# Seven block products for eight in the up-projections of a two-layer hybrid decoder, with weight sums made by adding DMAs

## The chip, the cores and the metric

The kernel runs on one core of one Trainium2 chip. Times are device microseconds of one execution of the whole program. The time before is 1455.77 us, the median of 3 runs (1455.77 to 1455.92). All arithmetic is float32; a matrix product is made of three passes in a rounded format, as told below.

## The reference, cut to what matters

Two decoder layers over 512 tokens of width 1024. Layer 0 mixes tokens by dilated window attention, layer 1 by a gated linear recurrence (LRU). After each mixer follows a gated feed-forward block, which the change is about:

```python
D_MODEL, SEQ, D_FF = 1024, 512, 3 * 1024

def rms_norm(x, g):
    return x * rsqrt(mean(x * x, axis=-1) + 1e-6) * g

def conv_ffn(x, w_up, conv_w, conv_b, w_down):          # w_up: 1024 x 6144
    u = causal_dwconv(x @ w_up, conv_w, conv_b)         # three taps over the tokens
    g, v = u[..., :D_FF], u[..., D_FF:]
    return (gelu(g) * v) @ w_down

for layer in range(2):
    h = mixer(rms_norm(x, norm_mix_pre[layer]))
    x = x + rms_norm(h, norm_mix_post[layer])
    h = conv_ffn(rms_norm(x, norm_ffn_pre[layer]), ...)
    x = x + rms_norm(h, norm_ffn_post[layer])
```

The product x @ w_up has two halves: 3072 features that go through gelu (gate) and 3072 that multiply them (value).

## The kernel before

The order of all work on each engine is the order in which the program writes it. Normalised activations stand transposed in SBUF as `hT`, 8 blocks of 128 input features by 512 tokens, split in two parts: `hi`, rounded to the matmul's format, and `lo`, the rest. Weights are split the same way. A product takes three passes, listed in `PASSES`: hi x hi, hi x lo, lo x hi (`mm3`, L259).

The up-projection of a layer (`ffn`) goes through 12 chunks j. For each j a chunk of 256 gate features and one of 256 value features is loaded (`w_cols`), 1 MB each. A chunk makes two tiles of 128 features by 512 tokens. For one tile, `feat` runs over 8 blocks of input features and 3 passes, 24 matmuls of 512 columns into one PSUM bank; chunk 0 of a layer does it in two halves of 256 columns, since the first tokens are ready earlier. `sink` then empties the bank: `conv` reads it three times, once on ACT (L596) and twice on DVE (L600, for the two shifted taps); a gate tile then gets its gelu on ACT (L611), a value tile is multiplied into it on DVE (L615). The down-projection (`rows_proj`) follows.

What feeds the matmuls is `pump`. A list `plan` holds all weight chunks of the program in order of use. Three buffers (`RAW_BUFS`) hold raw chunks; `load` issues the next load on SP's queue (L199) when one is free. `pump` cuts a raw chunk into pieces and splits each: ACT writes `whi` (L149), DVE writes `wlo` (L150), both 128 partitions by 512 elements at a time. At most 8 split units (`W_UNITS`) are alive. `tick`, called after every tile, pumps one or two pieces and advances the `side` generators, which hold work spread over several tiles, such as the norms. Since ACT and DVE work their queues in order, a split that waits for its data holds what is queued behind it.

`x_sb` holds the residual stream x in SBUF, 2 MB; `postnorm` adds to it after a projection. `gain` holds rows of norm gains, two buffers. PSUM has eight banks of 128 x 512, given out in turn.

Of the kernel before, what the change touches and what calls it, by code (L numbers as in the profile page):

```python
# [31 lines left out]

W_UNITS = 8
RAW_BUFS = 3
GEN_BUFS = 32
TOE_BUFS = 2
CP_PAD = 8
WARM = 5

SHORT_ORDER = [  # L40
# [34 lines left out]
def kernel(  # L75
# [29 lines left out]
    htp = ctx.enter_context(tc.tile_pool(name="htp", bufs=1))  # L105
    wp = ctx.enter_context(tc.tile_pool(name="wp", bufs=W_UNITS))
    gp = ctx.enter_context(tc.tile_pool(name="gp", bufs=GEN_BUFS))
# [6 lines left out]
    def nm(s):  # L114
        uid[0] += 1
        return f"{s}{uid[0]}"
# [13 lines left out]
    make_identity(nc, ident)  # L130
    x_sb = cp.tile([P, 4, D], F32, tag="x_sb", name="x_sb")

# [19 lines left out]
    plan = []  # L152
    state = {"dma": 0, "cv": 0, "live": 0, "next": 0, "hold": False}
    raws, units, pieces = {}, {}, []
    sides, first_w, first_y, one = [], [], [], []

    def parts_of(kind, raw):
# [7 lines left out]
        return [raw]  # L165

    def pump(limit=2):

        for _ in range(limit):
            i = state["cv"]  # L170
            if not pieces and i < state["dma"]:
                pieces.extend((i, j, u) for j, u in enumerate(parts_of(plan[i][0], raws.pop(i))))
                state["cv"] += 1
            if pieces and state["live"] < W_UNITS:
                i, j, raw = pieces.pop(0)
                hi, lo = (
                    wp.tile([P] + list(raw.shape[1:]), F32R, tag=t, name=nm("w" + t)) for t in ("hi", "lo")
                )
                h = raw.shape[1] // 2
                cuts = [(slice(None), slice(0, h)), (slice(None), slice(h, 2 * h))]  # L180
                if raw.shape[1] == 1:
                    cuts = [(slice(None), slice(0, 1), slice(n, n + 512)) for n in (0, 512)]
                if plan[i][4] is not None:
                    split_normed(hi, lo, raw, plan[i][4] + (2 * j if plan[i][0] == "value" else 0))
                    cuts = []
                for c in cuts:
                    split(hi[c], lo[c], raw[c])
                units[i, j] = (hi, lo)
                state["live"] += 1
            while not pieces and state["dma"] < len(plan) and state["dma"] - state["cv"] < RAW_BUFS:  # L190
                load()
# [17 lines left out]
    def take(i, j):  # L209
        while (i, j) not in units:  # L210
            before = state["live"]
            pump(1)
            assert before != state["live"]
        return units[i, j]

    def done(n=1):
        state["live"] -= n
# [4 lines left out]
    def tick():  # L222
        for s in list(sides):
            s[0] -= 1
            if s[0] <= 0:
                try:
                    s[0] = next(s[1])
                except StopIteration:
                    sides.remove(s)
        if not state["hold"]:  # L230
            pump(1 if state["live"] >= W_UNITS - 2 else 2)

# [3 lines left out]

    def w_cols(w, c0, normed=False):
# [4 lines left out]
        plan.append(("feat", KD, 256, srcs, 0 if normed else None))  # L242

# [71 lines left out]
    def prenorm(t, hT, g, wait):  # L315
        xh, gh = halves(x_sb[:, t, :]), halves(g)
# [31 lines left out]
    def first_transposed(t, i):  # L348

        ps = psum("tr")  # L350
        for k in range(4 * i, 4 * i + 4):
            nc.tensor.transpose(
                ps[:, k % 4 * P : (k % 4 + 1) * P],
                x_sb[:, t, i * 512 : i * 512 + 512].rearrange("t (p k) -> t k p", k=4)[:, k % 4], ident,
            )
        first_split(t, i, ps)
# [15 lines left out]
    def first_squares(i):  # L372
        for t in range(4):
            junk = gen(s="junk")
            nc.scalar.activation(
                junk, x_sb[:, t, i * 512 : i * 512 + 512], AF.Square, accum_out=first_ss[i][:, t : t + 1]
            )
# [22 lines left out]
    def postnorm(t, banks, g, final):  # L400
        at = [slice(0, 512), slice(512, 1024)]
        parts = banks
        u = [gen(s="post") for _ in at]

        def gained(i):
            nc.vector.tensor_tensor(u[i], parts[i], g[:, at[i]], op=ALU.mult)

        y = rms(parts, gained)
        for i, c in enumerate(at):
            xc = x_sb[:, t, c]  # L410
# [12 lines left out]
    def feat(W, hT, dst, n0, n1):  # L423
        for k in range(KD):
            mm3(
                dst[:, n0:n1],
                [w[:, k, :] for w in W],
                [h[:, k, n0:n1] for h in hT],
                k == 0,
                k == KD - 1,  # L430
            )

    def feat_tiles(n, hT, sink, halves=False):
# [15 lines left out]
        for c in range(n):  # L449
            i = chunk()  # L450
            for m in range(2):
                ps = psum()
                feat(take(i, m), hT, ps, 0, S)
                done()
                sink(2 * c + m, ps)
                tick()

# [17 lines left out]
    def rows_run(nchunks, A, prep, seq, order, post, pre, eng):  # L475
# [7 lines left out]
        def product(t, i, k, cols, start, stop):  # L483
            w = take(*W[k // 2][k % 2])
            c0 = i * 512
            mm3(
                banks[t][i][:, cols],
                [a[:, t * P : (t + 1) * P] for a in A[k]],
                [v[:, 0, c0 + cols.start : c0 + cols.stop] for v in w],
                start,  # L490
# [100 lines left out]
    def ffn(layer, hT, post, pre):  # L591
# [13 lines left out]
        gv = []  # L605

        def sink(b, ps, j):
            m = b % 2
            if b < 2:
                u = conv(ps, 2 * j + m)  # L610
                nc.scalar.activation(u, u, AF.Gelu_apprx_tanh)  # L611
                gv.append(u)
            else:
                u = conv(ps, 24 + 2 * j + m)
                nc.vector.tensor_tensor(gv[2 * j + m], gv[2 * j + m], u, op=ALU.mult)  # L615

        order = [([0, 1, 2, 3], range(9)), ([0], range(9, 12)), ([1], range(9, 12))]
        order += [([2, 3], [9]), ([2], [10, 11]), ([3], [10, 11])]
        prep, run = rows_proj(12, act_split(gv), order, post, pre)
        for j in range(12):  # L620
            if j == 11:
                prep(3)
            feat_tiles(2, hT, lambda b, ps: sink(b, ps, j), j == 0)
        return run()


    def attention(hT, post, pre):
# [50 lines left out]
        def first_values(vs):  # L678
# [4 lines left out]
            def product(t, u, which=range(6)):  # L683
                W = take(ids[u // 2], u % 2)
                steps = [(k, a, b) for a, b in PASSES for k in (2 * u, 2 * u + 1)]
                for n in which:
# [3 lines left out]
                        hT[a][:, k, t * P : (t + 1) * P],  # L690
                        W[b][:, k % 2, :],
                        start=u == n == 0,
# [22 lines left out]
            product(3, 1)  # L715
            done(2)
            first_split(2, 1, T[0])
# [8 lines left out]
            for t in range(4):  # L726
                product(t, 3)
                pump(1)
            done(2)
            for t in range(4):  # L730
# [14 lines left out]
        def values(vs, permute, midway=None):  # L745
# [6 lines left out]
            for t in range(4):  # L752
                banks[t] = psum("v")
                for u in range(4):
                    W = take(ids[u // 2], u % 2)
                    steps = [(k, a, b) for k in (2 * u, 2 * u + 1) for a, b in PASSES]
                    for k, a, b in steps:
                        mm(  # L758
                            banks[t],
                            hT[a][:, k, t * P : (t + 1) * P],  # L760
                            W[b][:, k % 2, :],
                            start=(k, a, b) == (0, 0, 0),
                            stop=(k, a, b) == (KD - 1, 1, 0),
                        )
                    if t == 3 and u % 2:
                        done(2)
                if permute:
# [189 lines left out]
    def lru(hT, post, pre):  # L957
# [19 lines left out]
        def gates(n):  # L977
            W = take(chunk(), 0)
            sg = {}
            for m in range(2):  # L980
                for gx in range(2):
                    ps = psum("gate")
                    for k in range(2):
                        mm3(ps, [w[:, 2 * gx + k, m * P : (m + 1) * P] for w in W], xs[2 * n + k], k == 0, k == 1)
                    j = 2 * n + m
# [78 lines left out]
    for layer in range(2):  # L1064
# [24 lines left out]
    def x_half(t, i):  # L1089
        c = slice(i * 512, (i + 1) * 512)  # L1090
        nc.sync.dma_start(x_sb[:, t, c], x[0, t * P : (t + 1) * P, c])

# [71 lines left out]
```

## Time and profile before

| | before |
|---|---|
| runs, us | 1455.77, 1455.92, 1455.77 |
| profiled execution: span, us | 1454.0 |
| granted TensorE clock | 0.999 |
| PE busy | 1445.0 us, 99% |
| DVE busy | 879.8 us, 61% |
| ACT busy | 675.9 us, 46% |
| POOL busy | 133.9 us, 9% |
| HBM read, written | 156.24 MB, 15.29 MB |

The page gives the profiled execution by its span, from the first to the last instruction; the median of the runs is 1.8 us (0.12%) above it. PE is the matmul engine, PEld its weight loads, which overlap with matmuls, DVE the vector engine, ACT the scalar engine, POOL GpSimd, SP the engine whose queue issues the weight loads. In a row for a group of instructions stand the line, engine and operation, the tiles (written <- read), shapes and count, then busy us in all and mean ns of one, then the engine's idle time ahead of them and what ended it. A row for a DMA ends with the size of one and the median us from issue to landing, where known.

### The profile page before, as it was taken

To read this page: it belongs to the slowest core of one execution; us is meant where nothing else is said; L and a number is where in the kernel's file an instruction comes from. 1 tells how busy PE (TensorE), PEld (TensorE's weight loads), DVE (VectorE), ACT (ScalarE), POOL (GpSimd) and SP (SyncE) were. 2 spreads that over 40 slices of the span, in tenths; PEclk is the share of its full clock that TensorE was granted. 3 is DMA by queue.
4 is the path that set the end of the run, shared out by engine and by line. 5 is a ranking of instruction groups with operands and counts; after the bars stand their busy time and mean duration, and the time that the engine had idled before them with its cause. 6 is when DMAs were issued, how large, how long until landed. Compare 5 with 4: busy or idle time off the path is not lost.

```text
span 1454.0 us, 18793 instructions
## 1 busy us (share of the span) xinstructions
PE 1445.0 (99%) x6861; PEld 1214.4 (84%) x6861; DVE 879.8 (61%) x1955; ACT 675.9 (46%) x1532; POOL 133.9 (9%) x275
## 2 busy tenths in 40 slices
PE   9999999999999999999999999999999999999998
PEld 7888888888888898888888888888898888888886
DVE  6767747474735975555564338769775555564333
ACT  7656636262615553343444335589453434444221
POOL 0340414040402100000000001000100000000000
PEclk9999999999999999999999999999999999999999
DMA  7653637372726343323323322432333233223201
GB/s 225 207 146 109 174 113 208 104 215 97 216 96 211 102 131 100 103 87 102 101 88 116 115 73 88 131 116 84 120 102 116 87 102 102 87 104 128 88 0 58
DMA packets 125364, 172.76 MB, mean 119 GB/s; under 512 B 8736, under 2 KB 102392, under 8 KB 125272
## 3 DMA queue, kind: packets, MB, share of 16 engines
q1 hardware_dynamic: 114280, 145.48, 31.0%
q0 software_dynamic: 10144, 25.04, 5.9%
q8 instruction: 54, 0.88, 0.2%
q10 hardware_dynamic: 848, 1.05, 0.2%
q14 instruction: 38, 0.31, 0.1%
HBM read 156.24 MB, written 15.29 MB: 118 GB/s over the span
## 4 chain that ended last, share of the span: by engine, by line
PE 93%; ACT 4%; DVE 3%; issue 1%; DVEq 0%; ACTq 0%
PE ps L259 55%; PE acc L259 24%; PE v L758 8%; PE v L688 1%; DVE xb L967 1%; PE O L909 1%; PE S L854 1%; PE S L808 1%; DVE wlo L150 1%; ACT sig L988 1%; ACT whi L149 1%; PE O L259 1%; PE tr L341 1%; ACT sig L1007 0%; ACT a L1005 0%
## 5 line engine op out<-in xcount | busy, mean ns | idle before, releaser
L259 PE MATMUL ps<-hT,whi 128*128 128x512 f32 (+1 forms) x2752 | 801.3, 375 | 0.0
L259 PEld LDWEIGHTS ps<-hT,whi 128*128 128x128 f32 x2752 | 503.6, 188 | 91.6
L259 PE MATMUL ps<-hT,wlo 128*128 128x512 f32 (+1 forms) x1376 | 515.3, 374 | 0.0
L150 DVE TENSOR_TENSOR wlo<-raw,whi 128x512 fp32r<-128x512 f32 x360 | 230.8, 686 | 187.2 <-ACT whi L149 187.1
L259 PEld LDWEIGHTS ps<-hT,wlo 128*128 128x128 f32 x1376 | 259.1, 188 | 46.5
L149 ACT ACTIVATE whi<-raw 128x512 fp32r<-128x512 f32 x360 | 204.6, 621 | 135.4 <-PE acc L259 121.0
L600 DVE SCALAR_TENSOR_TENSOR u<-ps,cols,u 128x511 f32<-128x511 f32 x192 | 143.8, 749 | 140.6 <-ACT u L596 137.2
L259 PE MATMUL acc<-whi,ahi 128*128 128x512 f32 x512 | 199.7, 390 | 0.0
L259 PE MATMUL acc<-whi,alo 128*128 128x512 f32 x512 | 199.4, 389 | 0.1
L259 PE MATMUL acc<-wlo,ahi 128*128 128x512 f32 x512 | 199.3, 389 | 0.0
L143 ACT ACTIVATE whi<-raw,first_w 128x128 fp32r<-128x128 f32 (+1 forms) x432 | 146.2, 425 | 56.6 <-PE ps L259 33.9
L596 ACT ACTIVATE u<-ps,cols 128x512 f32<-128x512 f32 x96 | 74.8, 779 | 210.0 <-PE ps L259 210.0
L144 DVE SCALAR_TENSOR_TENSOR wlo<-raw,first_w,whi 128x128 fp32r<-128x128 f32 (+1 forms) x432 | 139.5, 389 | 1.4 <-ACT whi L143 1.3
L259 PEld LDWEIGHTS acc<-whi,alo 128*128 128x128 f32 x512 | 96.1, 188 | 20.5 <-DVE alo L150 0.5
L259 PEld LDWEIGHTS acc<-whi,ahi 128*128 128x128 f32 x512 | 96.1, 188 | 19.8
L259 PEld LDWEIGHTS acc<-wlo,ahi 128*128 128x128 f32 x512 | 96.2, 188 | 19.8
L758 PE MATMUL v<-whi,hT 128*128 128x512 f32 x320 | 102.4, 393 | 0.0
L302 POOL DMA_DIRECT2D turned<-T x36 | 19.6, 547 | 763.4 <-DVE T L296 759.9
L309 POOL DMA_DIRECT2D ft<-turned x144 | 78.7, 554 | 39.6 <-issue 17.7
L758 PEld LDWEIGHTS v<-whi,hT 128*128 128x128 f32 x320 | 60.1, 188 | 12.3
L611 ACT ACTIVATE u<-u 128x512 f32<-128x512 f32 x48 | 30.3, 632 | 80.4 <-DVE u L600 80.4
L758 PE MATMUL v<-wlo,hT 128*128 128x512 f32 x160 | 62.3, 389 | 0.0
(171 smaller groups left out, 1010.7 us busy)
## 6 DMA issues: line engine op xcount, KB each, us to landing
raw<-in_ffn_w_up_dram SPq DMA_DIRECT2D x48, 1024.0 KB
raw<-in_attn_w_qkv_dram SPq DMA_DIRECT2D x67, 512.0 KB
raw<-in_ffn_w_down_dram SPq DMA_DIRECT2D x24, 1024.0 KB
raw<-in_lru_w_in_dram SPq DMA_DIRECT2D x8, 1024.0 KB
turned<-T POOLq DMA_DIRECT2D x28, 256.0 KB, 2.6
ft<-turned POOLq DMA_DIRECT2D x112, 64.0 KB, 5.8
vrows<-v SPq DMA_DIRECT2D x16, 256.0 KB
vp<-vrows SPq DMA_DIRECT2D x16, 256.0 KB
```

The source lines that it names most:

```text
L143: nc.scalar.activation(hi[:, k], raw[:, k], AF.Copy, scale=w)
L144: nc.vector.scalar_tensor_tensor(lo[:, k], raw[:, k], w, hi[:, k].bitcast(F32), op0=ALU.mult, op1=ALU.subtract)
L149: nc.scalar.activation(hi, raw, AF.Copy)
L150: nc.vector.tensor_tensor(lo, raw, hi.bitcast(F32), op=ALU.subtract)
L259: mm(dst, l[a], r[b], start=start and n == 0, stop=stop and n == 2)
L302: nc.gpsimd.dma_start(d, T)
L309: nc.gpsimd.dma_start(t[32 * c : 32 * c + 32].rearrange("j (b x) -> j b x", b=4), d.rearrange("(b j) (c x) -> c j b x", j=32, c=4)[c],)
L341: nc.tensor.transpose(ps[:, k * P : (k + 1) * P], xs[i][:, k * P : (k + 1) * P], ident)
L596: nc.scalar.activation(u, ps, AF.Identity, scale=cc[:, j : j + 1], bias=cc[:, 48 + j : 49 + j])
L600: nc.vector.scalar_tensor_tensor(u[:, d:], ps[:, : S - d], wc, u[:, d:], op0=ALU.mult, op1=ALU.add)
L611: nc.scalar.activation(u, u, AF.Gelu_apprx_tanh)
L758: mm(banks[t], hT[a][:, k, t * P : (t + 1) * P], W[b][:, k % 2, :], start=(k, a, b) == (0, 0, 0), stop=(k, a, b) == (KD - 1, 1, 0),)
```

## The change

For chunks 3 to 10 of both halves, in both layers (32 chunks of 48 matmuls of 512 columns), the product of the 1024 x 256 weights with the 512 tokens is done as two blocks by two by two: two groups of 128 output features, two halves of the input features (4 blocks of 128), two halves of the tokens (256). Instead of eight block products there are seven (Strassen's scheme in a form with sums of sums), each of 4 blocks x 3 passes = 12 matmuls of 256 columns. Five sides change with it:

* **Token sums.** Four combinations of the token blocks are made once per layer, in `token_sums`, a side generator that starts with chunk 1: `hi + lo` on POOL, four sums on DVE, splits on ACT and DVE. They need 2 MB and more of SBUF: x is written to memory, its place and that of the two gain rows are used for them, and `x_back` brings x back after chunk 10.
* **Weight sums.** Each chunk needs four blocks as they are or summed: `s1`, `s2`, `s3`, `s4` stand for sums made in place in the raw buffer by DMAs that add to their destination (`add_rows`, issued on POOL, 256 KB each, 512 bytes per row piece). `ahead` adds a block from memory onto another (S1), `across` adds the first block onto it (S2), `upper` makes S4 and S3. Four such DMAs per chunk. `stream` sets their order among the splits of successive chunks: each must come after the split that reads the old content and before the one that reads the sum.
* **Splits.** A chunk is split in seven pieces (S1, W12, W11, A22, S2, S4, S3) instead of four, of the same size. Units are counted in halves, 16 alive. A raw buffer is free when its chunk's S3 is split.
* **Chains.** `seven` writes products in slots; chunk n has its seven products at slots 7n + 0, 3, 4, 8, 9, 13, 19 (P5, P1, P3, P2, P6, P7, P4), so that up to three chunks overlap. `later` puts off what follows a product by one or two slots. Two PSUM banks collect a chunk: ACT copies an intermediate out twice and one back into PSUM negated, DVE makes two results of 256 columns in PSUM; then `finish` runs the same convolution as before. Empty slots at both ends are filled with quarters of ordinary tiles.
* **Elsewhere** units are lists of two halves instead of one tile; the instructions are the same.

Over the program 1536 matmuls of 512 columns are replaced by 2688 of 256 columns.

```diff
-W_UNITS = 8
+HALVES = 16
+SEVEN = range(3, 11)
+AT = {5: 0, 1: 3, 3: 4, 2: 8, 6: 9, 7: 13, 4: 19}
+HALF = ("s1", "w11", "w12", "a22", "s2", "s3", "s4")
...
+    def blocks(i):
+        raw = raws[i]
+        return {
+            n: raw[:, 4 * k : 4 * k + 4, m * P : m * P + P]
+            for n, m, k in (("w11", 0, 0), ("w12", 0, 1), ("s1", 1, 0), ("a22", 1, 1))
+        }
+    def add_rows(to, src):
+        nc.gpsimd.dma_start(to, src, accum_op=ALU.add)
+    def ahead(i):
+        add_rows(blocks(i)["s1"], plan[i][3][0][0][:, 4:8, P:256])
+    def stream(i0, n):
...
+            def upper(i=i):
+                x = blocks(i)
+                add_rows(x["w12"], x["s1"])
+                add_rows(x["w11"], plan[i][3][0][0][:, 0:4, P:256])
+            def across(i=i):
+                x = blocks(i)
+                add_rows(x["s1"], x["w11"])
+            for at, item in (
+                (-6.4, (None, lambda i=i: ahead(i))), (0, ("s1", "s1")), (0.2, (None, across)), (2, ("w12", "w12")),
+                (4, ("w11", "w11")), (4.2, (None, upper)), (6, ("a22", "a22")), (8, ("s2", "s1")),
+                (10, ("s4", "w12")), (12, ("s3", "w11")),
+            ):
...
+                    items.append((7 * c + at, item))
+        return [item for _, item in sorted(items, key=lambda x: x[0])]
...
-            while not pieces and state["dma"] < len(plan) and state["dma"] - state["cv"] < RAW_BUFS:
+            while state["dma"] < len(plan) and state["dma"] - state["used"] < RAW_BUFS:
                 load()
...
-        for j in range(12):
-            if j == 11:
-                prep(3)
-            feat_tiles(2, hT, lambda b, ps: sink(b, ps, j), j == 0)
+        for j in range(SEVEN[0]):
+            if j == 1:
+                side(token_sums(hT, T))
...
+        i = seven(hT, T, begin, i)
+        x_back()
+        prep(3)
...
+    def token_sums(hT, T):
+        d = dp.tile([P, 4, D], F32, name=nm("x_kept"))
+        nc.gpsimd.dma_start(d, X[0])
...
+            nc.gpsimd.tensor_tensor(o, hi.bitcast(F32), lo.bitcast(F32), op=ALU.add)
...
+            tt(b11, b11, b12, op=ALU.subtract)
+            tt(b12, b12, b22, op=ALU.subtract)
+            tt(b22, b22, b11, op=ALU.add)
+            tt(b21, b21, b22, op=ALU.subtract)
+            yield 1
+            for n, b in enumerate((b11, b22, b12, b21)):
+                split(homes[2 * n][k], homes[2 * n + 1][k], b)
...
+    LEFT = {5: ("s1", 1), 1: ("w11", 0), 3: ("s4", 1), 2: ("w12", 0), 6: ("s2", 1), 7: ("s3", 1), 4: ("a22", 1)}
+    def seven(hT, T, begin, before):
...
+                for k in range(4):
+                    for q, (wa, ha) in enumerate(PASSES):
+                        mm(
+                            y[b][:, 0:256], W[wa][0][:, k, :], right[n](ha, k), start=n in (1, 5) and k == q == 0,
+                            stop=k == 3 and q == 2, skip_group_check=True,
+                        )
+                done(1)
+                if n == 5:
+                    later(1, lambda: nc.scalar.activation(p5, c, AF.Copy))
+                elif n == 3:
+                    def seed():
+                        nc.scalar.activation(z, c, AF.Copy)
+                        nc.scalar.activation(c, a, AF.Copy, scale=-1.0)
+                    later(1, seed)
+                elif n == 6:
+                    later(1, lambda: nc.vector.tensor_tensor(y[0][:, 256:512], z, c, op=ALU.subtract))
+                    later(2, lambda: finish(b0, y[0], j))
+                elif n == 7:
+                    later(1, lambda: nc.vector.tensor_tensor(y[1][:, 256:512], c, p5, op=ALU.subtract))
+                elif n == 4:
+                    later(1, lambda: finish(b0 + 1, y[1], j))
...
+        at = {7 * n + AT[p]: f(p) for n, f in enumerate(chains) for p in AT}
+        after = chunk()
+        fill = quarters(before, 1, SEVEN[0] - 1, 3)
...
-            w_cols(ffn_w_up[layer], j * 256)
-            w_cols(ffn_w_up[layer], D_FF + j * 256)
+            for half in range(2):
+                w_cols(ffn_w_up[layer], half * D_FF + j * 256, kind="seven" if j in SEVEN else "feat")
```

More of the change, by code (lines that the diff above doesn't have):

```diff
@@ L165, in parts_of, with plain @@
         return [raw]
+    def plain(i, j, raw, last):
+        kind, k0 = plan[i][0], plan[i][4]
+        if kind == "rows":
+            cuts = [raw[:, :, n : n + 512] for n in (0, 512)]
+        else:
+            h = raw.shape[1] // 2
+            cuts = [raw[:, :h], raw[:, h:]]
+        norm = None if k0 is None else k0 + (2 * j if kind == "value" else 0)
+        return (i, j), lambda: cuts, norm, last
+    def blocks(i):
[4 more added lines that the diff above has]
+        }
@@ new lines, in refill @@
+    def refill():
+        i = state["cv"]
+        if i >= state["dma"]:
+            return
+        if plan[i][0] == "seven":
+            n = 1
+            while plan[i + n][0] == "seven":
+                n += 1
+            pieces.extend(stream(i, n))
+            state["cv"] += n
+        else:
+            if plan[i + 1 : i + 2] and plan[i + 1][0] == "seven":
+                pieces.append((None, lambda: ahead(i + 1)))
+            parts = parts_of(plan[i][0], raws[i])
+            pieces.extend(plain(i, j, r, j == len(parts) - 1) for j, r in enumerate(parts))
+            state["cv"] += 1
@@ L167, in pump @@
     def pump(limit=2):
         for _ in range(limit):
[L170 to L189, printed above, removed]
@@ L190, in pump @@
-            while not pieces and state["dma"] < len(plan) and state["dma"] - state["cv"] < RAW_BUFS:
+            if not pieces:
+                refill()
+            while pieces and pieces[0][0] is None:
+                pieces.pop(0)[1]()
+            if pieces and state["live"] + 2 - (pieces[0][0][1] in HALF) <= HALVES:
+                key, cuts, norm, last = pieces.pop(0)
+                cuts = cuts()
+                his, los = [], []
+                for n, raw in enumerate(cuts):
+                    hi, lo = (
+                        wp.tile([P] + list(raw.shape[1:]), F32R, tag=t, name=nm("w" + t)) for t in ("hi", "lo")
+                    )
+                    if norm is not None:
+                        split_normed(hi, lo, raw, norm + n * raw.shape[1])
+                    else:
+                        split(hi, lo, raw)
+                    his.append(hi)
+                    los.append(lo)
+                units[key] = (his, los)
+                state["live"] += len(cuts)
+                state["used"] += last
+                while pieces and pieces[0][0] is None:
+                    pieces.pop(0)[1]()
@@ L488, in product @@
                 [a[:, t * P : (t + 1) * P] for a in A[k]],
[L489 removed]
+                [v[i][:, 0, cols] for v in w],
                 start,
```

179 lines of the change are left out of this document (145 added, 34 removed).

## The prediction

> **What bounds the kernel now.** I read the busy shares first, then the chain that ended last, then the groups by shape, then the windows and the timeline of an up-projection.
>
> ```profile
> PE 1445.0 (99%) x6861; PEld 1214.4 (84%) x6861; DVE 879.8 (61%) x1955; ACT 675.9 (46%) x1532; POOL 133.9 (9%) x275
> PE 93%; ACT 4%; DVE 3%; issue 1%; DVEq 0%; ACTq 0%
> 510.00:764.00 254.00, 254.00 (x1181) 212.93 (x1180) 151.59 (x223) 107.38 (x177) 0.00 (x0) 1.00 0.31 101
> ```
>
> TensorE is busy for 99% of the span and is 93% of the chain. The third line is the window 510 to 764 us, nearly all of layer 0's up-projection: span, then PE, PEld, DVE, ACT and POOL busy, granted clock (1.00), DMA share (0.31) and GB/s (101). PE never rests; DVE works 60% of that stage, ACT 42%, POOL nothing. So only less TensorE time can shorten the stage, and the question is whether what is added elsewhere still fits beside it.
>
> A busy sum does not give the rate of matmuls that overlap; the chain in order of time does (start, us, count):
>
> ```profile
> 31.98 27.20 PE ps L259 x120
> 510.50 253.77 PE ps L259 x1176
> 500.13 5.75 PE ps L259 x48
> 902.35 2.87 PE ps L259 x24
> ```
>
> The first piece is all 512 columns wide: 27.20/120 = 0.2267 us per matmul. The last two are stretches where chunk 0 runs in two halves of 256 tokens: 5.75/48 = 0.1198 and 2.87/24 = 0.1196. The second piece is layer 0's remaining 120 narrow and 1056 wide ones, and fits: (253.77 - 120 x 0.1198)/1056 = 0.2267. A half-width matmul thus costs 53% of a wide one, about 13 ns on each being independent of width.
>
> **The TensorE term.** A chunk (256 output features of one half) now takes 48 wide matmuls: 48 x 0.2267 = 10.88 us. As seven products it takes 7 x 12 = 84 narrow ones: 84 x 0.1198 = 10.06 us, 1.44 us per product. Both layers have 32 such chunks: 1536 wide matmuls go (348.2 us), 2688 narrow come (322.0 us): **-26.2 us**. That is 7.5% of those matmuls and not the eighth that the count suggests. The Trainium skill, "TensorE: Matmul & The Clock Gate", section "Back-to-back issue gap", has width/2.4 + 2.5 ns, an estimate of 109 and 216 ns, by which the saving would be 38 us; the rows above are slower at both widths, so the sum goes by them.
>
> **DVE and ACT per chunk period of 10.06 us.** Rows by shape, and two by time:
>
> ```profile
> L150 DVE TENSOR_TENSOR wlo<-raw,whi 128x512 fp32r<-128x512 f32 x360 | 230.8, 686 | 187.2 <-ACT whi L149 187.1
> L149 ACT ACTIVATE whi<-raw 128x512 fp32r<-128x512 f32 x360 | 204.6, 621 | 135.4 <-PE acc L259 121.0 <-PE ps L259 14.4
> L596 ACT ACTIVATE u<-ps,cols 128x512 f32<-128x512 f32 x96 | 74.8, 779 | 210.0 <-PE ps L259 210.0
> L600 DVE SCALAR_TENSOR_TENSOR u<-ps,cols,u 128x511 f32<-128x511 f32 x96 | 71.9, 749 | 137.2 <-ACT u L596 137.2
> L615 DVE TENSOR_TENSOR u<-u,u 128x512 f32<-128x512 f32 x48 | 33.2, 692 | 1.6
> L611 ACT ACTIVATE u<-u 128x512 f32<-128x512 f32 x48 | 30.3, 632 | 80.4 <-DVE u L600 80.4
> L842 DVE TENSOR_TENSOR o<-O,o 128x384 f32<-128x384 f32 x8 | 4.4, 556 | 3.7 <-ACT o L841 3.7
> L821 ACT ACTIVATE L<-L,s 128x256 f32<-128x256 f32 x24 | 11.8, 494 | 0.0
> L143 ACT ACTIVATE whi<-raw,first_w 128x128 fp32r<-128x128 f32 x384 | 115.2, 390 | 24.1 <-PE ps L259 24.1
> 561.22 1.29 DVE L150 TENSOR_TENSOR wlo<-raw,whi 128x512 fp32r<-128x512 f32 x2 [1.28 <-ACT whi L149]
> 552.96 1.53 DVE L600 SCALAR_TENSOR_TENSOR u<-ps,cols,u 128x511 f32<-128x511 f32 x2 [1.98 <-ACT u L596]
> ```
>
> A chunk's weights were split in four pieces and now in seven. DVE: seven splits at 0.686, four convolution steps at 0.749, half a gate product (0.692), and the two new 256-column subtractions, estimated at 0.43 each (0.556 at 384 columns and 0.686 at 512 put a column at 1.0 ns). Sum 4.80 + 3.00 + 0.35 + 0.86 = 9.0 us as a mean; a value chunk has the whole product, 9.35. Back to back two splits take 1.29, so 4.5 instead of 4.8 is possible. ACT: 7 x 0.621 + 2 x 0.779 + 0.32 + three 256-column copies at about 0.45 (between the 128- and 256-column rows) = 7.6 us. So DVE comes to 90% and ACT to 76%: they fit, DVE barely. The order is periodic (14 products), so I expect no queueing at 90%. Each of the in-between copies must finish within 3 products (4.3 us) after its source is complete, for which one queued split and one operation suffice.
>
> **The DMAs.** Each period adds four transfers of 256 KB in rows of 512 bytes that add into the weight buffer, all issued on POOL, which is idle here. No row shows an adding DMA. Nearest:
>
> ```profile
> turned<-T POOLq DMA_DIRECT2D x28, 256.0 KB, 2.6
> ft<-turned POOLq DMA_DIRECT2D x112, 64.0 KB, 5.8
> raw<-in_ffn_w_up_dram SPq DMA_DIRECT2D x48, 1024.0 KB
> SPq L199 <- DVE wlo L150: 893.9, 88, 23.8
> ```
>
> Rate: the window's 254 us x 101 GB/s are 24.5 loads of 1 MB, and 254 x 0.31 = 78.7 us of all 16 engines, 3.2 us a load. At that rate per byte an add costs 0.8 us as a plain copy, 1.6 if the destination has to be read too. At the other end each 512-byte row costs as much as a 1 KB row and is read twice: 3.2. So DMA per period is 3.2 + 4 x (0.8 to 3.2) = 6.4 to 16.0 us against 10.06. I take 1.6, 9.6 us, since the row nearest in kind (256 KB from POOL) lands in 2.6 us all told. "Collectives: The Full Stack" in the Trainium skill, "The bandwidth ceiling: the fold count and why AG ≠ RS ≠ AR", says that an adding transfer runs at half a copy's rate for its two source reads; by that the add is again 1.6 us, an estimate. No run here shows it yet, and what short rows add stays open.
>
> Latency: an add lands in 2.6 us (the same size) to 5.8 us (the same 512 row pieces). A load takes 3.2 + (2.6 - 0.8) = 5.0. There are three weight buffers, and the last split of a chunk frees its own for the chunk three later. From there run load, the add into S1, then (the program's order on DVE) six splits, two convolutions and one subtraction until the split that frees the buffer of two periods later: 0.62 + 6 x 0.645 + 2 x 1.53 + 0.43 = 8.0 us. So two periods take at least 5.0 + 5.8 + 8.0 = 18.8 us; 20.1 are there, 1.3 to spare. Before, loads waited for free buffers (the SP row), with time to spare.
>
> **Around the chains.** Per layer the token sums add 16 DVE operations (eight sums, eight splits), eight ACT ones and eight sums on POOL (no row; POOL has the 38 us of seven tiles for them): DVE gets some 16 x 0.69 = 11 us more in a stretch where it idles 40%: hidden. The last four token splits, however, are queued behind the convolution of the tile just finished, and the first product needs one of them:
>
> ```profile
> 552.15 0.78 ACT L596 ACTIVATE u<-ps,cols 128x512 f32<-128x512 f32 x1 [3.62 <-PE ps L259]
> ```
>
> From the tile's end: 0.78 ACT, 1.53 and 0.69 DVE, one split 0.65 = 3.65 us, less the six matmuls that can go ahead (0.72): 2.9 us of idle PE. The third product, P3, needs S4's split, ninth on DVE behind that one: 3.65 + 9 x 0.65 = 9.5 us, where PE would be at 3.65 + 0.72 + two quarter tiles (12 x 0.2267) + P1 (1.44) = 8.5: another 1 us. Of these 3.9 I take 3.5 us per layer, **+7 us** (bounds 0 and 10). The end has no such hole: eight quarter tiles fill the empty slots. The stream of x to memory and back (2 MB each way, 6.4 us of DMA each) lies beside chunks 1 and 2 and the down-projection; the first reader of x comes after it. Changed unit sizes elsewhere (attention, LRU) move no instruction: zero, within 1 us either way.
>
> **Sum.** Span 1454.0 us, 1.8 below the runs' median 1455.77, which I take as a constant. 1455.8 - 26.2 + 7 = 1436.6. For handshakes and DMA collisions in the chains I add 5 us (0.15 us per chunk; bounds 0 and 14): **1442 us**.
>
> **The rivals.**
> *The adds cost rate (slower).* If 512-byte rows are dear, the DMA engines set the period: beyond 1.7 us per add (3.2 + 4 x 1.7 = 10), and the whole gain is gone at about 1.87. For it: nothing before moved such rows twice. Against: 2.6 us to landing with latency in it. Midway, 2.4 us per add: period 12.8, 32 x (12.8 - 10.88) + 7 = +68, 1524 us.
> *The three buffers' loop.* If load and add, sharing the engines, take over 12.1 us together (20.1 - 8.0), DVE stands at S1's split with all behind it, convolutions included. With each 1.6 us later: (6.6 + 7.4 + 8.0)/2 = 11.0 us: +3.8 + 7, 1467 us. For it: only 1.3 us to spare. Against: that margin used the longest latency.
> *DVE takes over.* If both convolutions wait uncovered for ACT's 0.78 us (in the timeline DVE idles 1.98 before each): 9.35 + 1.56 = 10.9 us, 1463 us. Against: a split is queued between. A mild form at 10.65 is no change.
>
> **How the numbers follow.** About 0.2% (3 us) is what measurement tells from no change. Forecast (period up to 10.57): 0.56, its own range 1434 (start cost 4 us, nothing else) to 1453. Adds at their rate: 0.16. Loop: 0.12. DVE: 0.16, of which 0.05 is no change. So faster 0.56, same 0.05, slower 0.39. The range leaves out the rate rival and little else: 1434 to 1482.
>
> **What would show it.** In the changed profile: 84 narrow matmuls per chunk in 10.1 us (a longer period is a wait, named by who released PE: DVE or ACT splits whose own wait is a DMA speak for the loop; a DMA share above 0.9 with PE idle for the rate rival; DVE at 95% for the third). Two holes of about 3 us on PE at the first product. ACT near 76%, DVE near 90% in the stage. A narrow matmul above 0.1296 us (10.88/84) would void the whole gain.

## The result and the profile after

The change makes the kernel slower: 1516.22 us, median of 4 runs (1513.36 to 1528.6), against 1455.85 us for the kernel before (1455.77 to 1456.03): ratio 1.0431 [1.0393, 1.0469]. The forecast was 1442 us with a range of 1434 to 1482, so it missed by 74 us and on the wrong side.

The profiled execution took 1513.36 us with a span of 1511.5. Its busy shares and the chain's shares:

```profile
PE 1443.9 (96%) x8013; PEld 1265.1 (84%) x8013; DVE 1001.2 (66%) x2147; ACT 769.5 (51%) x1740; POOL 321.4 (21%) x423
PE 64%; DMA 16%; DVE 11%; ACT 6%; issue 2%; POOL 1%; DVEq 0%; ACTq 0%; POOLq 0%
```

TensorE was 93% of the chain and is 64%. DMA, which the chain of the kernel before did not contain at all, is 16%. The windows show where (layer 0's up-projection: start of the chains, middle, end; then the middle of layer 1's). The columns are window, span, then PE, PEld, DVE, ACT and POOL busy, granted clock, DMA share, GB/s:

```profile
515.00:577.00 62.00, 50.86 (x264) 43.26 (x263) 51.81 (x63) 28.35 (x48) 22.26 (x18) 0.92 0.60 139
606.00:750.00 144.00, 125.48 (x999) 123.68 (x998) 101.26 (x165) 79.02 (x153) 57.87 (x45) 0.96 1.01 174
1160.00:1330.00 170.00, 154.90 (x1195) 151.78 (x1194) 117.88 (x191) 92.20 (x178) 71.25 (x55) 0.95 1.00 176
```

In the middle stretches the packets' times add up to the whole time of the 16 DMA engines (share 1.01 and 1.00, it was 0.31) while PE idles 13% and 9% of it and DVE 30%. PE also idles 11 us at the start of the chains. Its granted clock, 1.00 before, is 0.92 to 0.96 in these stretches.

A share near 1 looks like full engines, and I read it so at first. It is a mean, and packet times overlap. In single microseconds of the same stretch it goes from 0.00 to 1.44:

```profile
634.00:635.00 1.00, 1.00 (x6) 1.00 (x6) 1.00 (x2) 0.22 (x1) 1.00 (x2) 0.50 0.00 0
642.00:643.00 1.00, 1.00 (x11) 1.00 (x10) 0.96 (x2) 0.00 (x0) 0.17 (x1) 1.00 1.44 179
```

In the first the engines move nothing. In the second only adding DMAs are under way (the last load before it has landed, the next goes at 645.03), and they pass at 179 GB/s, which is 256 KB in 1.5 us.

The middle of the stage in the chain, in order of time (start, us, what):

```profile
609.21 9.50 DMA raw<-in_ffn_w_up_dram
618.71 0.02 issue
618.73 0.64 ACT whi L152
619.37 0.02 issue
619.39 0.69 DVE wlo L153
620.09 0.35 DVE ps L833
620.44 0.34 issue
620.78 9.22 DMA raw<-raw
...
634.35 9.28 DMA raw<-in_ffn_w_up_dram
```

PE is not in this piece. A chain of adds carries the time: an add from memory (9.50 us), its split on ACT and DVE, a result on DVE, an add from SBUF to SBUF (9.22), splits, and the next. From one add from memory to the next on the chain is 25.1 us, about two chunk periods. The view names the last event before each step; by the program the add at 620.78 (S4) also needs the sum S2, whose add went at 612.16 and landed after 8.0 us. So adds wait for adds. One buffer's turn shows it in full: its load, then the adds S1, S2 and S3, then the next load into it (the S3 line is the chain's, with its time to landing):

```profile
635.31 0.37 SPq L275 DMA_DIRECT2D raw<-in_ffn_w_up_dram  x1
642.83 1.28 POOL L190 DMA_DIRECT2D raw<-in_ffn_w_up_dram  x1 [4.28 <-DMA raw<-in_ffn_w_up_dram]
649.28 1.29 POOL L190 DMA_DIRECT2D raw<-raw  x1 [0.98 <-DVE wlo L153]
658.33 10.04 DMA raw<-in_ffn_w_up_dram
669.78 0.37 SPq L275 DMA_DIRECT2D raw<-in_ffn_w_up_dram  x1
```

That is 34.5 us, and three buffers give three periods for it. The queue of loads gives the period itself: SP's row in the timeline covers eleven loads from the first issue to the last, ten periods.

```profile
610.19 121.20 SPq L275 DMA_DIRECT2D raw<-in_ffn_w_up_dram  x11
```

That is 12.1 us per chunk instead of the 10.06 of the forecast, or the 10.88 of the kernel before.

What an adding DMA costs, which no row of before could tell, follows from the queue that POOL issues (packets, MB, share of 16 engines' span), here in the changed kernel and then in the same kernel without its 128 adds (1447.3 us of span, told below):

```profile
q0 software_dynamic: 78304, 66.99, 25.6%
```

```profile
q0 software_dynamic: 10720, 33.43, 7.3%
```

0.256 x 1511.5 - 0.073 x 1447.3 = 387.0 - 105.7 = 281.3 us of packet time, spread over 16 engines, for 128 adds: **2.20 us of packet time per add of 256 KB**. Since packets overlap, this is more than the 1.5 us at which adds pass one after the other. The landing times are in the page's list of DMA issues (count, KB each, median us from issue to landing):

```profile
raw<-in_ffn_w_up_dram POOLq DMA_DIRECT2D x64, 256.0 KB, 5.8
raw<-raw POOLq DMA_DIRECT2D x64, 256.0 KB, 7.2
```

### The profile page after: what moved, and what is told of

The parts are those of the page before. It is cut to its first block, busy times and chain, and to the rows that moved or that the text cites. A ratio compares the mean times of both kernels' runs of the same rounds, so it can differ in the third digit from the quotient of the medians.

```text
span 1511.5 us, 22098 instructions
## 1 busy us (share of the span) xinstructions
PE 1443.9 (96%) x8013; PEld 1265.1 (84%) x8013; DVE 1001.2 (66%) x2147; ACT 769.5 (51%) x1740; POOL 321.4 (21%) x423
## 4 chain that ended last, share of the span: by engine, by line
PE 64%; DMA 16%; DVE 11%; ACT 6%; issue 2%; POOL 1%; DVEq 0%; ACTq 0%; POOLq 0%
PE ps L335 24%; PE acc L335 23%; DMA raw<-in_ffn_w_up_dram 8%; DMA raw<-raw 8%; PE v L1002 7%; DVE wlo L153 5%; PE ps L815 4%; ACT whi L152 2%; DVE u L678 2%; PE v L932 2%; DVE xb L1211 1%; PE O L1153 1%; PE S L1098 1%; PE S L1052 1%; ACT sig L1232 1%
## 5 line engine op out<-in xcount | busy, mean ns | idle before, releaser
L335 PE MATMUL ps<-hT,whi 128*128 128x512 f32 (+1 forms) x1728 | 488.8, 369 | 0.0
L153 DVE TENSOR_TENSOR wlo<-raw,whi 128x512 fp32r<-128x512 f32 x456 | 321.7, 733 | 234.7 <-ACT whi L152 234.3
L335 PE MATMUL ps<-hT,wlo 128*128 128x512 f32 (+1 forms) x864 | 317.2, 367 | 0.0
L815 PE MATMUL ps<-T,whi 128*128 128x256 f32 x1024 | 197.2, 291 | 33.1 <-ACT T L152 14.9
L815 PEld LDWEIGHTS ps<-T,whi 128*128 128x128 f32 x1024 | 166.7, 199 | 37.4 <-ACT T L152 16.1
L335 PEld LDWEIGHTS ps<-hT,wlo 128*128 128x128 f32 x864 | 163.6, 189 | 27.1
L815 PE MATMUL ps<-hT,whi 128*128 128x256 f32 x768 | 146.8, 291 | 25.9 <-ACT ps L826 25.9
L815 PE MATMUL ps<-T,wlo 128*128 128x256 f32 x512 | 148.2, 289 | 0.0
L190 POOL DMA_DIRECT2D raw<-in_ffn_w_up_dram x64 | 101.3, 1583 | 172.0 <-DMA raw<-in_ffn_w_up_dram 87.3
L190 POOL DMA_DIRECT2D raw<-raw x64 | 82.0, 1282 | 152.0 <-DVE wlo L153 89.1
```

Source lines behind the costliest of these rows:

```text
L153: nc.vector.tensor_tensor(lo, raw, hi.bitcast(F32), op=ALU.subtract)
L190: nc.gpsimd.dma_start(to, src, accum_op=ALU.add)
L335: mm(dst, l[a], r[b], start=start and n == 0, stop=stop and n == 2)
L815: mm(y[b][:, 0:256], W[wa][0][:, k, :], right[n](ha, k), start=n in (1, 5) and k == q == 0, stop=k == 3 and q == 2, skip_group_check=True,)
```

## The experiments

The theory after this result had three parts. The *rate*: four adds at 2.2 us and a load of 3.4 need 12.2 us of the DMA engines per chunk. The *loop*: with three weight buffers a load can start only when the buffer's last split is done, and load, add and splits in series take longer than two periods. The *start*: eight token sums on POOL hold DVE. The rivals were the loop alone without a limit of rate, DVE being full, and PE's slower clock. All kernels ran beside the kernel before, which took 1455.8 to 1455.9 us in every group.

### Without the adds

```diff
 def add_rows(to, src):
-    nc.gpsimd.dma_start(to, src, accum_op=ALU.add)
+    return
```

> All four adding transfers per chunk are left out, so the weight sums are not formed; every matmul, split and copy stays. The changed kernel has a period of 12.1 us per chunk, DMA share 1.0. Theory 1 (the adds' engine time sets the period: 4 x 2.16 us beside 3.55 us of load): the period falls to TensorE's 10.06 us, 32 x 2.04 = 65 us less, 1451 us, DMA share about 0.35. Theory 2 (latency of load and adds in the loop of three buffers): the same 1451 us. Theory 3 (DVE and ACT handshakes): the period stays above 10.5 us, 1465 us or more.

Measured: 1449.04 us (one run). Loads and a window of the stage:

```profile
603.22 110.35 SPq L275 DMA_DIRECT2D raw<-in_ffn_w_up_dram  x12
570.00:720.00 150.00, 148.94 (x1208) 147.43 (x1209) 126.51 (x205) 101.87 (x189) 0.00 (x0) 0.98 0.34 110
```

Eleven periods in 110.35 us are 10.0 us each, the forecast's 10.06. DVE is busy 84%, ACT 68%: neither is the bound (both theories of the adds expected this), and the seven products are as cheap as they were costed. The adds cost 1516.2 - 1449.0 = 67 us. What is left above 1455.8 - 26.2 = 1429.6 is 19 us, of which the mended start, below, takes 17. A load takes 0.34 x 150 / 15 = 3.4 us of packet time.

### Four weight buffers

```diff
-RAW_BUFS = 3
-GEN_BUFS = 32
+RAW_BUFS = 4
+GEN_BUFS = 28
```

The fourth buffer takes the place of four working tiles.

> Four raw weight buffers for three; 28 general tiles for 32 make the room. Theory 1 (engine time of the adds): period 12.1 us and DMA share 1.0 as before, 1510 to 1520 us. Theory 2 (latency in the loop): a load can start a period earlier, 10 us more slack, so the period falls to TensorE's 10.06 us, about 1451 us, with DMA share 1.0 no longer held.

Measured: 1493.39 us (one run).

```profile
609.55 112.58 SPq L275 DMA_DIRECT2D raw<-in_ffn_w_up_dram  x11
606.00:740.00 134.00, 121.98 (x1004) 119.81 (x1002) 100.72 (x163) 78.70 (x151) 58.20 (x45) 1.00 1.06 186
```

The period falls from 12.1 to 11.3 us and stays there, with the DMA share at 1.06 and PE idle 9%. Neither theory holds alone: the fourth buffer was worth 0.9 us per chunk, and something else holds the period at 11.3. The share of 1.06 points at the rate; the run with four adds below shows why that is not enough. PE's clock is back at 1.00 in this window, and PE still waits: a period above 10.06 does not need the slower clock. How much of the 0.9 us the clock gave was not separated.

### Adds on half of the columns

```diff
-    nc.gpsimd.dma_start(to, src, accum_op=ALU.add)
+    nc.gpsimd.dma_start(to[:, :, 0:64], src[:, :, 0:64], accum_op=ALU.add)
```

> Each adding transfer takes only the first 64 of 128 columns: as many rows, 256 bytes instead of 512 each (half of each weight sum is not formed). If an adding row costs by bytes (67 ns per 512, so 34 per 256): an add takes 1.08 us, DMA work 3.55 + 4.3 = 7.9 us per chunk, TensorE sets the period again, 1451 us. If a row costs the same whatever its length (67 ns): no change, 1516 us. In between the DMA share tells the row's price.

Measured: 1474.31 us (one run). Row pieces of 256 instead of 512 bytes, as many as before:

```profile
q0 software_dynamic: 78304, 50.21, 20.7%
609.11 121.48 SPq L275 DMA_DIRECT2D raw<-in_ffn_w_up_dram  x12
```

0.207 x 1472.4 - 105.7 = 199.1 us for 128 adds: 1.56 us for half the bytes, 71% of 2.20. So of the packet time of a 256 KB add in 512 row pieces about 0.9 us does not depend on bytes and 1.3 us does (2.20 - 2 x (2.20 - 1.56) = 0.92; two points, taken as a line). It is neither a price per byte nor one per row. The period is 11.0 us although the packet times come to only 3.4 + 4 x 1.56 = 9.6: here waits in series are the bound, not the amount.

### The token sums on DVE, and earlier

```diff
-            nc.gpsimd.tensor_tensor(o, hi.bitcast(F32), lo.bitcast(F32), op=ALU.add)
+            nc.vector.tensor_tensor(o, hi.bitcast(F32), lo.bitcast(F32), op=ALU.add)
```

In the changed kernel's timeline at the start of the chains (start, us, engine, line, operation, tiles, count):

```profile
528.91 12.00 DVE L153 TENSOR_TENSOR wlo<-raw,whi 128x512 fp32r<-128x512 f32 x2
529.82 10.53 POOL L744 TENSOR_TENSOR B<-hT,hT 128x512 f32<-128x512 f32 x8
572.32 0.58 PE L815 MATMUL ps<-T,whi 128*128 128x256 f32 x1 [6.55 <-ACT T L152]
576.26 0.58 PE L815 MATMUL ps<-T,whi 128*128 128x256 f32 x1 [3.36 <-DVE T L153]
```

Two splits that take 1.29 us elsewhere take 12.00, during the whole of POOL's eight sums. Everything on DVE is late by that, and PE waits 6.55 and 3.36 us for token splits.

> The eight sums hi + lo of the token blocks go from POOL to DVE (same operation). In the changed kernel one DVE split lasted 11.4 us while POOL made its eight sums (10.5 us), and the first product then waited 11 us per layer. Theory A (DVE with two SBUF inputs is held while POOL reads SBUF): no split over 0.8 us, the hole at the first product falls to the 3 to 4 us of the prediction, 2 x 7 = 14 us less, about 1502 us. Theory B (the hole comes from DVE's amount of work or from the DMAs then): no less hole, 1516 us or up to 10 us more.

Measured: 1502.51 us (1501.45 to 1504.07), ratio 1.0318 [1.0301, 1.0335], as expected. The splits by line (count: min/median/max ns), first in the changed kernel, then here:

```profile
L153 DVE TENSOR_TENSOR wlo<-raw,whi x456: 648/685/11420, 415.9 to 1462.0; 128x512 fp32r<-128x512 f32 x152
```

```profile
L153 DVE TENSOR_TENSOR wlo<-raw,whi x456: 649/685/695, 415.9 to 1452.7; 128x512 fp32r<-128x512 f32 x152
```

The longest split falls from 11.42 us to 0.695, and 13.7 us of the total go with it. PE's waits for the token splits in layer 0 (released by: us, times, longest) were 11.1 us in the changed kernel

```profile
PE ps L815 <- ACT T L152: 7.4, 2, 6.6
PE ps L815 <- DVE T L153: 3.7, 2, 3.4
```

and are 4.4 here:

```profile
PE ps L815 <- DVE T L153: 3.4, 1, 3.4
PE ps L815 <- ACT T L152: 1.0, 1, 1.0
```

With `yield 2` after these sums made `yield 1`, so that the rest starts a step earlier:

> As with the token sums on DVE (1502.5 us), and each step of the token sums one tile earlier, so that the first product's token block is split before the tile ahead of it ends. Two waits of 3.6 us for it are left there. If those cost time: 2 x 3.5 = 7 us less, 1495 us. If the adding transfers set the end of the stage whatever comes before (the chunks' weights being late by then), nothing: 1502 us.

Measured: 1504.49 us (one run): no gain beside the 1502.51. PE's waits for the token splits fell to 1.8 us, but PE then waited elsewhere, as the second theory had it.

### One add fewer by DMA, then two

```diff
-                add_rows(x["s1"], x["w11"])
+                nc.vector.tensor_tensor(x["s1"], x["s1"], x["w11"], op=ALU.add)
```

> On top of that, the addition that makes S2 (both operands in the raw buffer) is done by DVE, 128 x 512 elements, 0.65 us per chunk; three adding transfers stay. Theory 1 (engine time): 3 x 2.16 + 3.55 = 10.0 us per chunk against TensorE's 10.06, the period falls from 12.2 to 10.1 to 10.5: 1432 to 1445 us. Theory 2 (only the latency of two adding transfers in series per two chunks counts): one of the two is gone, the same or better, 1432 us. Theory 3 (DVE has no room: 8.4 us per chunk without adds, 9.05 with one): if its order costs more than that, above 1450 us.

Measured: 1482.76 us (1480.49 to 1487.6), ratio 1.0195 [1.0178, 1.0213]: a miss. In addition:

```diff
-                add_rows(x["w12"], x["s1"])
+                nc.vector.tensor_tensor(x["w12"], x["w12"], x["s1"], op=ALU.add)
```

> As the kernel with one addition on DVE, and the addition that makes S4 on DVE too; two adding transfers stay, both from memory. DMA work 2 x 2.16 + 3.55 = 7.9 us per chunk, DVE 8.4 + 2 x 0.63 = 9.7 us, TensorE 10.06. Theory 1: the period is TensorE's, 1430 to 1436 us, faster than the kernel before by 1.4 to 1.8%. Theory 3: DVE at 97% sets a period of 10.2 to 10.6, 1436 to 1450 us.

Measured: 1478.53 us (1476.21 to 1481.63), ratio 1.0157 [1.0141, 1.0172]: a miss too, and the more telling one.

```profile
605.97 126.56 SPq L275 DMA_DIRECT2D raw<-in_ffn_w_up_dram  x12
600.00:740.00 140.00, 129.48 (x1060) 127.80 (x1059) 119.55 (x196) 83.98 (x162) 29.72 (x23) 0.99 0.68 143
```

The DMA engines are at 0.68, DVE at 85%, and the period is still 11.5 us. Nothing is full, so something goes round. One turn from the trace: a load is issued at 651.04, the add onto its block goes at 660.18 and lands at 664.72, the split of it runs on DVE at 665.40, at 674.60 DVE ends the last split that frees a buffer, and the next load goes at 674.62. That is 23.6 us, two periods of 11.8 here. The add and the split of that turn in the chain:

```profile
660.18 4.54 DMA raw<-in_ffn_w_up_dram
...
665.40 0.70 DVE wlo L153
```

Fewer adds relieve the DMA engines, but a load and an add in series are still too long for three buffers.

### Both: fewer adds and four buffers

The same two kernels with `RAW_BUFS = 4`, `GEN_BUFS = 28`; first with two adds on DVE:

> Two additions on DVE, two adding transfers, early token sums, and four raw weight buffers (28 general tiles). With three buffers the period was 11.75 us at a DMA share of 0.67: load 9.1 us from issue to landing beside the adds, the add into S1 4.5, then 8 us of splits and convolutions, 2 periods = 23 us. Loop theory: with four buffers the same 22 to 23 us may take 3 periods, so TensorE's 10.06 us sets the period: 1430 to 1437 us, faster than before by 1.3 to 1.8%. Rate theory (DMA engines): the share was 0.67, so nothing else may bind there. DVE theory: 8.4 + 1.3 us per chunk leave nothing, the period stays at 10.4 to 11, 1440 to 1460 us.

Measured: 1439.32 us (1438.16 to 1440.03), ratio 0.9888 [0.9871, 0.9904]. With one add on DVE:

> As the kernel with two additions on DVE and four buffers, with one of them (S4) an adding transfer again: DMA work 3.55 + 3 x 2.16 = 10.0 us per chunk against TensorE's 10.06, DVE 9.05. If the DMA engines can be kept full (four adds and four buffers gave a share of 1.06 to 1.10 and 11.2 us per chunk): 1430 to 1440 us. If the loop's latency binds at that load: 10.5 to 11, 1445 to 1460 us.

Measured: 1438.1 us (1436.41 to 1438.34), ratio 0.9875 [0.9861, 0.989], the fastest kernel of the study. Its loads, and windows of it and of the kernel with two on DVE:

```profile
608.25 90.40 SPq L275 DMA_DIRECT2D raw<-in_ffn_w_up_dram  x10
600.00:720.00 120.00, 120.00 (x1010) 120.00 (x1009) 109.97 (x180) 84.97 (x156) 39.76 (x31) 1.00 0.96 185
```

```profile
600.00:720.00 120.00, 120.00 (x1010) 120.00 (x1009) 115.70 (x192) 82.78 (x158) 25.74 (x20) 1.00 0.74 161
```

Nine periods in 90.40 us are 10.04 us: PE never waits in the window, in either. With three adds the packet times come to 3.4 + 3 x 2.2 = 10.0 us per chunk, a share of 0.96. DVE holds out at 92% and even at 96% without a wait on PE, so the order in which the work is queued leaves no gaps that matter.

### Each cause by itself

No adds, with the start mended (token sums on DVE, `yield 1`):

> No weight sums at all (they are left out), three buffers, token sums on DVE and a tile earlier. What is left is the matmuls, splits and copies: if TensorE's rate is the only limit then, 1455.8 - 26.2 = 1429.6 us; each hole at the start of the chains that is left adds its length twice.

Measured: 1431.91 us (one run), 2.3 above the expected.

```profile
600.00:720.00 120.00, 120.00 (x1010) 120.00 (x1010) 103.43 (x168) 85.34 (x156) 0.00 (x0) 1.00 0.35 115
```

All four adds by DMA, four buffers, the start mended:

> All four adding transfers as in the change, four buffers, token sums on DVE and a tile earlier. Rate theory: with the loop's wait gone the DMA engines set the period: 11.2 us as with four buffers alone, share above 1; 32 x (11.2 - 10.06) = 36 us above the 1432 us without adds, 1468 us, between 1462 and 1480. If latency was all of it: 1432 to 1440 us.

Measured: 1481.28 us (1480.31 to 1484.2), ratio 1.0178 [1.0163, 1.0193], 1 us beyond the rate theory's range.

```profile
601.93 111.91 SPq L275 DMA_DIRECT2D raw<-in_ffn_w_up_dram  x11
600.00:720.00 120.00, 112.99 (x920) 111.26 (x919) 94.50 (x154) 74.27 (x143) 55.60 (x43) 0.99 1.07 188
```

The share is 1.07 and the period 11.2 us. Against the fastest kernel the only difference is that the fourth add goes by DMA and not on DVE, 32 times: 43 us. But that this is the engines' rate is not shown. In this kernel, too, they stand still in between:

```profile
646.00:647.00 1.00, 1.00 (x11) 1.00 (x9) 1.00 (x3) 0.94 (x3) 1.00 (x2) 1.00 0.00 1
```

The trace shows a round in POOL's queue instead. The add that makes S2 goes at 648.57, S1's add of the next chunk right behind it at 649.32, although the load under it was issued at 634.78; it lands after 9.3 us, beside the other adds, is split, and only then can that chunk's S2 add go, at 660.34: 11.8 us after the first. With S2's sum on DVE this round is gone, and 2.2 us of packet time as well; the runs do not separate the two. S1's add issued earlier, or a fifth buffer, was not tried. These runs add up the whole change (the 1431.9 and the 1504.5 are single ones):

| Kernel | us | step |
|---|---|---|
| before | 1455.9 | |
| seven products, start mended, no adds | 1431.9 | -24 |
| with four adds per chunk by DMA, four buffers | 1481.3 | +49 (adds waiting for adds, and their amount) |
| three buffers | 1504.5 | +23 (loop) |
| the change (token sums on POOL, a step later) | 1516.2 | +12 (start) |

32 chunks at 11.2 instead of 10.04 us are 37 of the 49; the other 12 were not traced one by one (PE idles also at both ends of the stages there, 2.7 us of the 30 before the window and 4.7 of the 40 after it).

### The rest of the start

In the fastest kernel PE still waited 4.0 us for token splits. Left out: the step between the two halves of the token sums.

```diff
-            if not k:
-                yield 1
```

> As the kernel with one addition on DVE and four buffers (1438.1 us), and the second half of the token sums directly after the first, one tile earlier still. That kernel's first product still waits 2.4 us per layer for its token block. If that is what is left above the 1432 us without weight sums: 4 to 5 us less, 1433.5 us. If DVE, busier there, is late with something else instead: 1438 us.

Measured: 1441.12 us (1440.42 to 1442.24), ratio 0.9897 [0.988, 0.9913]: no gain, 3 us more than the kernel it was to mend. The waits there (engine, what, released by: us, times, longest):

```profile
PE ps L813 <- ACT part L819: 7.3, 2, 3.7
```

The wait for the token splits is gone and another of 3.7 us per layer has come: ACT's first copy of an intermediate is queued behind the splits that were moved ahead of it.

## Why the prediction was wrong, point by point

* **TensorE term: right.** -26.2 us forecast, -24 measured in the kernel without adds. A piece of the changed kernel's chain (start, us, count) has the same price as before, 0.1191 us for a narrow matmul:

```profile
587.80 17.15 PE ps L815 x144
```

The saving of 38 us that the Trainium skill's formula would give ("TensorE: Matmul & The Clock Gate", "Back-to-back issue gap"; the page gives it for an isolated matmul) did not appear in any run.

* **DVE and ACT: right.** 9.0 us of DVE per chunk were forecast; 103.43/120 of a period of 10.04 are 8.7. ACT: 7.6 forecast, 85.34/120 make 7.1. The new 256-column subtractions took 0.42 us (0.43 forecast). The rival in which DVE takes over, given 0.16, did not happen even with a 256 KB sum added to its queue.

```profile
L830 DVE TENSOR_TENSOR ps<-part,ps 128x256 f32<-128x256 f32 x32 | 13.5, 422 | 0.2 <-PE ps L815 0.2
```

* **The DMAs' rate: not shown to have failed.** I took 1.6 us for an add between bounds of 0.8 and 3.2. Its packet time was 2.20, past the 1.87 us at which, by the prediction's own figure, the whole gain is gone. But that figure counts an engine as taken by one packet at a time, and where only adds were under way they passed in 1.5 us each. At that price four adds and a load are 4 x 1.5 + 3.4 = 9.4 us, an estimate, close to the 9.6 of the forecast and under TensorE's 10.06. The rate rival's 1524 us was the nearest number to what came, but by luck: it has engines that never rest, and no loop. The rule of the Trainium skill ("Collectives: The Full Stack", "The bandwidth ceiling: the fold count and why AG ≠ RS ≠ AR"), half a copy's rate, was the other support of 1.6. The page works it out for the ReduceScatter of a ring, not for a single adding DMA; the trace agrees with it here, 179 GB/s for adds alone against 355 for a load alone (605 to 607 us of the kernel without adds).

* **The latency of the adds, and the loop of three buffers: the step that failed.** The forecast set 5.0 (load) + 5.8 (add) + 8.0 against 20.1. In four turns of the changed kernel S1's add went 7.5 to 9.1 us after its load was issued, since the load shares the engines with other adds, and landed 4.6 to 5.2 us after that: 12.2 to 14.3 us in place of 10.8, and over the 12.1 at which, by the prediction's own rival, the loop binds. Even with half of the adds gone load and add took 13.7 us. And the forecast had one add in the loop, where three follow each other in a buffer: S2's needs S1's, S4's needs S2's, and S3's stands in POOL's queue behind S4's. It put that series at nothing; with landings of 4.5 to 10.0 us it makes the 34.5 us of the turn above, against 30.2 in three periods of 10.06. The sentence that the margin "used the longest latency" was the mistake: the longest latency of a row in which the engines were at a share of 0.31 is no bound for one in which they carry three times as much. The loop rival, given 0.12, had the mechanism: its 6.6 + 7.4 = 14.0 us for load and add are about what came. Its 1467 us was too little because it, too, counted one add, and because of the start.

* **Start of the chains: 3.5 us per layer forecast, 11.1 measured in layer 0.** The hole that the prediction worked out is the 4.4 us that are left with the sums on DVE. The step that failed is the one that called POOL's eight sums hidden: POOL had the time, but while it read SBUF a two-input operation of DVE stood still.

* **Handshakes: right.** With buffers and adds out of the way 5 us were allowed for and 2 (no adds) appeared. The end of the chains had its own holes only where the adds ran late.

Both signs that the prediction had named appeared, the DMA share above 0.9 with PE idle and splits that wait for a DMA. The first was meant for the rate rival and came without engines that are always at work. The second, in the waits of the changed kernel (us, times, longest):

```profile
ACT whi L152 <- DMA raw<-in_ffn_w_up_dram: 64.3, 32, 5.0
ACT whi L152 <- DMA raw<-raw: 57.0, 14, 6.6
```

The rivals were priced as if one of them would happen. The loop and the start happened together, and with a fourth buffer the adds' round in POOL's queue, which no rival had, took the loop's place. The loop alone (1478.5 us with two adds) and the four adds alone (1481.3 us with four buffers) were each enough to lose the gain.

## What to carry to other kernels

An operation of which the profile has no row deserves a run of its own before it is put four times into every period, and a loop must be counted with every one of them that follows another: here one was counted and there were three. A DMA share is a sum of packet times; near 1 it does not say that the engines are full, and single microseconds tell. A latency read where the DMA engines are a third busy says nothing about a loop that runs while they carry three times as much, so give such a loop a spare buffer. When two limits lie close together, mending one of them shows nothing: fewer adds alone (1.0157) and more buffers alone (1493 us) both still lost, together they gained 1.1 to 1.2%.

## What the hardware showed that I had not expected

* An adding DMA of 256 KB in row pieces of 512 bytes took 2.20 us of packet time over the 16 engines, one of 128 KB in as many pieces 1.56. Packets overlap: in a microsecond with adds alone the share was 1.44 and 179 GB/s passed. An add landed 4.5 to 10.0 us after its issue, beside other adds and loads.
* POOL's eight two-input sums on SBUF (10.53 us) held one two-input operation of DVE for 11.4 us, the whole train and not one instruction. The Trainium skill, "SBUF — State Buffer", "Who interferes with whom", says that a DVE instruction with two SBUF inputs contends with a GpSimd instruction that reads SBUF. The trace agrees, and adds that DVE did not get in between eight of them issued back to back, although the record of its split starts at 529.51, before POOL's first sum at 529.82.
* PE's granted clock was 0.92 to 0.96 in stretches of the changed kernel in which PE idled in holes of some 3 us, and 1.00 in the window of the kernel with four buffers alone, where it idled 9%. In one such hole PE did nothing from 628 to 631 us, and from 633 to 635 us its clock was 0.50. What lowers it was not tested.
